# First block's norms on the vector engine, first weights in tiles of their own, and four casts with a fixed place in ScalarE's order

## The chip, the cores and the metric

One NeuronCore of a Trainium2 chip runs the kernel. The metric is the device time of one execution in microseconds. The engines are named as in the profile: PE (TensorE), DVE (VectorE), ACT (ScalarE), POOL (GpSimd) and SP, whose queue issues every DMA of this kernel.

## The reference, cut to what matters

One decoder layer over 2048 tokens of width 1024, in float32:

```python
h = rmsnorm(x, g_mix)                       # x * rsqrt(mean(x^2) + 1e-6) * g_mix
z = h @ w_in                                # 1024 x 4352: r|k|v, three loras, pool, two gates
z_rwkv = token_shift(z[..., :1792], mu)     # z + (z_prev - z) * mu
y_a = rwkv7_mix(z_rwkv, ...) @ w_out_a      # loras, delta-rule state, group norm
y_b = multiscale_pool_mix(z_pool) @ w_out_b
x = x + (gate_a * y_a + gate_b * y_b) @ w_o
x = x + square(relu(rmsnorm(x) @ w_ff1)) @ w_ff2
x = x + sigmoid(rmsnorm(x) @ w_pg) * (p @ w_pe)
return rmsnorm(x, g_final)
```

The change touches the first two lines, for the first 512 tokens.

## The kernel before

The tokens are cut into four blocks of 512. `stage_A(b)` norms a block, turns it (transposes it through PE into `big`), multiplies it by `w_in` in column blocks of 128 and works the results up; `stage_B(b)` does the two output projections; the MLP and the embedding follow. Between the dense work run the recurrent units (`prep`, `chain`, `gnorm`). They read what `stage_A` stored in `zD`, and the first may begin when block 0's twelve r, k, v column blocks are stored.

A float32 product is made of three products of halves (`mm3`): a tile is split into a high half, which ACT makes by a rounding copy ("CAST" in the profile), and a low half, the difference, which DVE or POOL makes. `transpose_split` does it for the turned input, `wtile` for the weights: it loads a 512 KB column block into a `wr` tile (four buffers), casts it into a `wf` tile (three buffers, L241) and subtracts (L244, DVE 384 columns, POOL 640). With `keep` it also stores the split block and enters it in the table `wcache`, so that a later block loads it ready made. For block 0 that is done for column blocks of even number.

Ahead of `stage_A` the first block's four tiles of 128 tokens are loaded into the same four `wr` buffers and normed (L214 to L225): ACT sums the squares, `rstd` is 13 small operations on DVE, and the scaling follows. For x0 and x1 DVE does it in one operation (L222); for x2 and x3 POOL multiplies by the gain `gmix` (L224) and DVE by the statistic (L225). The first weights, column block 12, are then asked for by `wtile` (all of their low half on POOL). They take the `wr` buffer of x0, so their load waits until x0 has been turned.

The order of work: PE's instructions stand in program order. Those of the other engines and of SP are ordered by the library, by priority (program order) and by a simulated time line of the kernel. In `stage_A(0)` the program order is: turn x0 and x1; first half (256 tokens) of column block 12; turn x2 and x3; turn the small vectors (`fill_vec`); second half of block 12; its shift, tanh and casts into `yx`; block 13; its shift, tanh and cast into `yx`; then blocks 0 to 11, each with a small lora product and a tanh behind it. The blocks are generators, and `wtile` is called for a block when its generator is first advanced, after the lines that stand before it have been traced:

```python
            zl = yield from shifted(12, 12)        # block 12: product, copy out (L457), shift
            ...
                ACT.copy(out=yx[on, 0, i, :], in_=src[on])                     # L472, twice
            zl = yield from shifted(13, 13)        # calls wtile for block 13 first
            ...
            ACT.copy(out=yx[:, 0, 2, :], in_=zl)                               # L478
            for zi, m in enumerate(zorder):
                zs = yield from shifted(zi, m)     # calls wtile for block m first
                ...
                    ACT.activation(out=lo, in_=ps, func=AF.Tanh, ...)          # L491
```

Of the kernel before, what the change touches and what calls it, by code (L numbers as in the profile page):

```python
# [10 lines left out]
F32 = mybir.dt.float32  # L11
FR = mybir.dt.float32r
# [3 lines left out]
ALU = mybir.AluOpType  # L16
AX = mybir.AxisListType

P = 128
# [14 lines left out]
TB = 512  # L34
# [64 lines left out]
def hybrid_kernel(ctx, tc, consts, x, p, g_mix, w_in, mu_shift, w0, w_decay_up, a0, w_aaa_up,  # L99
                  w_gate_up, k_k, k_a, r_k, ln_x_w, ln_x_b, pool_w, pool_scale, b_gates,  # L100
                  w_out_a, w_out_b, w_o, g_mlp, w_ff1, w_ff2, g_ple, w_ple_gate, w_ple_proj,
                  g_final, out, stop=None, dbg=None):
    nc = tc.nc
    PE, ACT, DVE, POOL, SP = nc.tensor, nc.scalar, nc.vector, nc.gpsimd, nc.sync
# [5 lines left out]
    dram = ctx.enter_context(tc.tile_pool(name="dram", bufs=1, space=bass.MemoryType.DRAM))  # L110
# [6 lines left out]
    const = ctx.enter_context(tc.tile_pool(name="const", bufs=1, side="left"))  # L117
# [26 lines left out]
    def rsqrt(pool, src, n, tag, iters=3, rows=P, bufs=2):  # L144

        y = pool.tile([rows, n], F32, name=f"rs_y{tag}", bufs=bufs)
        h = pool.tile([rows, n], F32, name=f"rs_h{tag}", bufs=bufs)
        q = pool.tile([rows, n], F32, name=f"rs_q{tag}", bufs=bufs)
        DVE.tensor_scalar(y.bitcast(I32), src.bitcast(I32), 1, None, op0=ALU.logical_shift_right)
        DVE.tensor_scalar(y.bitcast(I32), y.bitcast(I32), -1.0, MAGIC, op0=ALU.mult, op1=ALU.add)  # L150
        DVE.tensor_scalar(h, src, -0.5, None, op0=ALU.mult)
        for _ in range(iters):
            DVE.tensor_tensor(q, y, y, ALU.mult)
            DVE.tensor_tensor(q, q, h, ALU.mult)
            DVE.scalar_tensor_tensor(y, q, 1.5, y, op0=ALU.add, op1=ALU.mult)
        return y

    def sumsq(pool, xt, ss, junk_kw):
        junk = pool.tile([P, D], BF16, name="junk", **junk_kw)
        ACT.activation(out=junk, in_=xt, func=AF.Square, accum_out=ss)  # L160

    def rstd(pool, ss, n, tag):

        ms = pool.tile([P, n], F32, name=f"nms{tag}", bufs=2)
        DVE.tensor_scalar(ms, ss, 1.0 / D, 1e-6, op0=ALU.mult, op1=ALU.add)
        return rsqrt(pool, ms, n, tag)
# [34 lines left out]
    with ExitStack() as c1:  # L201
        fg = c1.enter_context(tc.tile_pool(name="fg", bufs=1, side="left"))
        c1r = ExitStack()
        const = c1r.enter_context(tc.tile_pool(name="const1", bufs=1, side="left"))

        def load_x(b, j):
            xt = fg.tile([P, D], F32, name="xt", tag="wr", bufs=WR)
            SP.dma_start(out=xt, in_=xv[b * TB + j * P:b * TB + (j + 1) * P, :])
            return xt


        gbc = const.tile([P, D], F32, name="gmix")
        xnext = {}
        for j in range(4):  # L214
            xnext[0, j] = load_x(0, j)
            if j == 0:
                SP.dma_start(out=gbc, in_=g_mix[0].unsqueeze(0).broadcast_to([P, D]))
            r = fg.tile([P, 1], F32, name="xss0", bufs=4)
            sumsq(fg, xnext[0, j], r, dict(tag="t2k", bufs=5))
            r = rstd(fg, r, 1, "n")  # L220
            if j < 2:
                DVE.scalar_tensor_tensor(xnext[0, j], xnext[0, j], r, gbc, op0=ALU.mult, op1=ALU.mult)  # L222
            else:
                POOL.tensor_tensor(xnext[0, j], xnext[0, j], gbc, ALU.mult)  # L224
                DVE.tensor_scalar(xnext[0, j], xnext[0, j], r, None, op0=ALU.mult)  # L225

        wcache = {}

        def wtile(src, k, n, ws=WS, key=None, keep=False):


            if key in wcache:
                wf = fg.tile([P, 2, 1024], FR, name="wf", tag="wf", bufs=3)
                SP.dma_start(out=wf.bitcast(F32), in_=wcache[key])
                return wf.rearrange("p s (k n) -> p s k n", n=n)
            raw = fg.tile([P, 1024], F32, name="wr", tag="wr", bufs=WR)
            rv = raw[:, 0:k * n].rearrange("p (k n) -> p k n", n=n)
            SP.dma_start(out=rv, in_=src)
            wf = fg.tile([P, 2, 1024], FR, name="wf", tag="wf", bufs=3)
            hi = wf[:, 0, 0:k * n]  # L240
            ACT.copy(out=hi, in_=raw[:, 0:k * n])  # L241
            for eng, c in ((DVE, slice(0, ws)), (POOL, slice(ws, 1024))):
                if c.start < c.stop:
                    eng.tensor_tensor(wf[:, 1, c], raw[:, c], hi.bitcast(F32)[:, c], ALU.subtract)  # L244
            if keep:
                wcache[key] = dram.tile([P, 2, 1024], F32, name=f"wc{len(wcache)}")
                SP.dma_start(out=wcache[key], in_=wf.bitcast(F32))
            return wf.rearrange("p s (k n) -> p s k n", n=n)
# [2 lines left out]

            return b == i % 2

        winv = w_in[0].rearrange("(k p) c -> p k c", p=P)
        wpre = wtile(winv[:, :, 12 * P:13 * P], 8, P, 0, ("in", 12 * P), True)

        cst = const.tile([P, C_MK - P], F32, name="cst")
        SP.dma_start(out=cst, in_=consts[:, P:C_MK])
# [50 lines left out]
        for i in range(2):  # L309
            raw = fg.tile([P, RW], F32, name="lraw", tag="t2k", bufs=5)  # L310
# [24 lines left out]
        raw = fg.tile([P, 2 * P], F32, name="craw", tag="t2k", bufs=5)  # L335
# [71 lines left out]
        def stage_A(b, nxt):  # L407
            t0 = b * TB
            hT = big
            def proj(ps, c0, lo_last=False, wf=None, cols=slice(0, TB)):  # L410
                if wf is None:
                    wf = wtile(winv[:, :, c0:c0 + P], 8, P, key=("in", c0), keep=kept(b, c0 // P))
                if lo_last:
                    for w, h in ((0, 0), (1, 0), (0, 1)):
                        for k in range(8):
                            mm(ps[:, cols], wf[:, w, k, :], hT[:, h, k, cols], (w, h, k) == (0, 0, 0), (h, k) == (1, 7))
                            if k % 3 == 2:
                                yield
                    return
                for k in range(8):  # L420
                    mm3(ps, (wf[:, 0, k, :], wf[:, 1, k, :]), (hT[:, 0, k, :], hT[:, 1, k, :]), k == 0, k == 7)
                    yield
# [130 lines left out]
            for m in range(8):  # L553
                if m >= 1:
                    next(ah, None)
                if m < 7 or not to_B:
                    yield from gate_a(m)
                if m < 7 and prods:
                    yield from product(*prods.pop(0))
                elif pend:  # L560
                    pool_tail(*pend.pop(0))
                    yield
                ps = dps()
                for i, _ in enumerate(proj(ps, 3328 + m * P)):
                    if m == 7 and i == 2:
                        next(ah, None)
                    yield
                th = t2k()
                ACT.activation(out=th, in_=ps, func=AF.Tanh, bias=bgh[:, 8 + m:9 + m], scale=0.5)
                while pend:  # L570
                    pool_tail(*pend.pop(0))
                    yield
                if m % 2 == 0:
                    wob = wtile(wbv[:, :, m * P:(m + 2) * P], 4, 2 * P, key=("b", m), keep=kept(b, m // 2))
                prods.append((m, wob, th))
# [677 lines left out]
    raw = f2.tile([P, 1024], F32, name="wr", tag="wr", bufs=3)[:, 0:512].rearrange("p (k n) -> p k n", n=P)  # L1253
# [114 lines left out]
    lo, hi = slice(0, 512), slice(512, D)  # L1368
# [83 lines left out]
    for n, (blk, c, nm) in enumerate(seq):  # L1452
# [25 lines left out]
        for j in range(4):  # L1478
# [7 lines left out]
            s = {k: v[j] for k, v in accs.items()}  # L1486
# [180 lines left out]
```

## Time and profile before

| | |
|---|---|
| median of 3 runs | 3246.0 us (3239.34 to 3246.55) |
| profiled execution | 3245.66 us |
| its span, first to last instruction | 3243.9 us |
| PE busy | 3046.2 us (94%) |
| DVE, ACT, POOL busy | 2478.3, 1393.3, 1232.9 us |
| mean granted clock of PE | 0.974 of full speed |

The span is what the rows below are counted in, from its start. A row of a time line gives start, length, engine, line of the kernel, operation, the tile written and the tiles read, with a count where several were merged; in brackets is the idle time in front of it and what ended it.

### The profile page before, as it was taken

To read this page: it belongs to the slowest core of one execution; us is meant where nothing else is said; L and a number is where in the kernel's file an instruction comes from. 1 tells how busy PE (TensorE), PEld (TensorE's weight loads), DVE (VectorE), ACT (ScalarE), POOL (GpSimd) and SP (SyncE) were. 2 spreads that over 40 slices of the span, in tenths; PEclk is the share of its full clock that TensorE was granted. 3 is DMA by queue.
4 is the path that set the end of the run, shared out by engine and by line. 5 is a ranking of instruction groups with operands and counts; after the bars stand their busy time and mean duration, and the time that the engine had idled before them with its cause. 6 is when DMAs were issued, how large, how long until landed. Compare 5 with 4: busy or idle time off the path is not lost. (4 is left out here: it accounts for less than half of the span.)

```text
span 3243.9 us, 43606 instructions
## 1 busy us (share of the span) xinstructions
PE 3046.2 (94%) x14409; PEld 2487.0 (77%) x14409; DVE 2478.3 (76%) x5419; ACT 1393.3 (43%) x2697; POOL 1232.9 (38%) x1325
## 2 busy tenths in 40 slices
PE   7999998899999998879979999999989999999998
PEld 6777777778787876758768788788768888887787
DVE  4479887788888888985478787866658898888765
ACT  4445654455445544533144444433343335333332
POOL 4555444444343534531125555645422232222100
PEclk9999999999999999989999999999989999999999
DMA  7866767666666666767765556544454456435431
GB/s 245 245 218 209 237 208 229 228 218 207 210 224 208 203 193 221 256 217 253 278 214 170 187 187 227 196 152 150 181 205 145 154 191 220 147 117 178 142 108 69
DMA packets 422846, 636.50 MB, mean 196 GB/s; under 512 B 173726, under 2 KB 286044, under 8 KB 391388
## 3 DMA queue, kind: packets, MB, share of 16 engines
q1 hardware_dynamic: 422620, 633.72, 58.9%
q8 instruction: 114, 1.87, 0.2%
q14 instruction: 112, 0.92, 0.1%
HBM read 439.62 MB, written 193.99 MB: 195 GB/s over the span
## 5 line engine op out<-in xcount | busy, mean ns | idle before, releaser
L133 PE MATMUL d<-big,wf 128*128 128x512 f32 (+1 forms) x3288 | 851.5, 407 | 19.5 <-DVE wf L244 9.4
L133 PEld LDWEIGHTS d<-big,wf 128*128 128x128 f32 x3288 | 610.7, 193 | 158.4 <-DVE wf L244 12.2
L133 PE MATMUL d<-op 128*128 128x512 f32 x1344 | 318.6, 396 | 18.9 <-ACT op L1111 14.8
L1112 POOL TENSOR_TENSOR op<-hr,op 128x1024 fp32r<-128x1024 f32 x56 | 157.2, 2807 | 455.4 <-ACT op L1111 455.4
L133 PEld LDWEIGHTS d<-op 128*128 128x128 f32 x1344 | 254.3, 189 | 78.3 <-ACT op L1111 15.2
L1111 ACT CAST op<-hr 128x1024 fp32r<-128x1024 f32 x112 | 117.7, 1051 | 357.3 <-issue 151.8
L1112 DVE TENSOR_TENSOR op<-w,op 128x1024 fp32r<-128x1024 f32 x112 | 183.6, 1640 | 109.3 <-ACT op L1111 109.3
L872 DVE TENSOR_TENSOR Xtmp<-Xt,At 128x16 f32<-128x16 f32 (+15 forms) x512 | 239.9, 468 | 9.3
L1112 POOL TENSOR_TENSOR op<-wr,op 128x512 fp32r<-128x512 f32 x96 | 145.9, 1521 | 246.7 <-ACT op L1111 246.6
L133 PE MATMUL d<-wf,big 128*128 128x512 f32 x768 | 202.3, 416 | 21.0 <-DVE t2k L611 18.7
L133 PE MATMUL d<-yx,wf 128*128 128x512 f32 x768 | 205.4, 413 | 15.7 <-DVE t2k L611 6.5
L1293 POOL TENSOR_TENSOR t<-t,t 128x512 f32<-128x512 f32 x128 | 192.2, 1511 | 69.0 <-DVE t L1303 31.6
L133 PEld LDWEIGHTS d<-wf,big 128*128 128x128 f32 x768 | 147.6, 198 | 59.7 <-DVE t2k L611 22.9
L133 PE MATMUL d<-wg,op 128*128 128x512 f32 x768 | 184.2, 395 | 4.5 <-ACT wg L1111 3.1
L133 PEld LDWEIGHTS d<-yx,wf 128*128 128x128 f32 x768 | 146.1, 197 | 51.9 <-DVE t2k L611 8.2
L1111 ACT CAST op<-wr 128x512 fp32r<-128x512 f32 x192 | 114.7, 619 | 155.4 <-DMA wr<-in_w_ff_dram 39.8
L133 PEld LDWEIGHTS d<-wg,op 128*128 128x128 f32 x768 | 145.1, 190 | 38.5 <-ACT wg L1111 5.7
L133 PE MATMUL rp<-op 128*128 128x512 f32 x672 | 171.3, 390 | 0.0
L133 PE MATMUL rc<-op 128*128 128x512 f32 x672 | 170.6, 389 | 0.0
L875 DVE TENSOR_REDUCE Xt<-Xtmp 128x8 f32<-128x16 f32 (+15 forms) x512 | 147.4, 288 | 9.2
L244 POOL TENSOR_TENSOR wf<-wr,wf 128x640 fp32r<-128x640 f32 (+2 forms) x69 | 119.9, 1739 | 78.5 <-ACT wf L241 73.1
L133 PEld LDWEIGHTS rp<-op 128*128 128x128 f32 x672 | 126.1, 188 | 26.9
(320 smaller groups left out, 6322.3 us busy)
## 6 DMA issues: line engine op xcount, KB each, us to landing
wf<-wc SPq DMA_DIRECT2D x131, 1024.0 KB, 5.3
wc<-wf SPq DMA_DIRECT2D x50, 1024.0 KB, 6.2
wr<-in_w_ff_dram SPq DMA_DIRECT2D x64, 512.0 KB, 3.8
w<-in_w_ff_dram SPq DMA_DIRECT2D x32, 1024.0 KB, 7.5
wr<-in_w_in_dram SPq DMA_DIRECT2D x51, 512.0 KB, 4.4
zD<-t2k SPq DMA_DIRECT2D x96, 256.0 KB, 3.9
zs<-zD SPq DMA_DIRECT2D x32, 640.0 KB, 6.4
At<-aD SPq DMA_DIRECT2D x32, 512.0 KB, 4.8
```

What stands on the lines that cost most here:

```text
L133: PE.matmul(out_, lhsT, rhs, start=start, stop=stop, **kw)
L244: eng.tensor_tensor(wf[:, 1, c], raw[:, c], hi.bitcast(F32)[:, c], ALU.subtract)
L872: DVE.tensor_tensor(tmp[:, :, :, 0:n], Xt[:, :, 0:n].unsqueeze(2).broadcast_to([P, MCOL, FS, n]), At[:, 0:n, r:n].rearrange("p s r -> p r ...
L875: DVE.tensor_reduce(Xt[:, :, r:n].unsqueeze(3), tmp[:, :, :, 0:n], AX.X, ALU.add)
L1111: ACT.copy(out=dst[0], in_=src)
L1112: eng.tensor_tensor(dst[1], src, dst[0].bitcast(F32), ALU.subtract)
L1293: eng.tensor_tensor(out_, a, b, op)
```

## The change

The four sums of squares are asked for first, and the statistics and scalings come behind them in order: x0, x1, then x2 and x3 with one set of statistics for both. All four scalings are one DVE operation each, and POOL has no part. The weights of column block 12 are loaded in two halves of 256 KB into two tiles of their own (buffers that the `ze` tiles use later), behind x1 on SP's queue; each half is cast by ACT and subtracted by DVE, and the split block is stored and entered in the table as before.

In `wtile`, a cast that is traced while the table holds at most two entries is handed to `tc.keep_in_program_order`. That library function adds one edge of order, from the instruction that was traced last before it on the same engine to this one. The edge fixes the order of issue, and adds no wait of its own. The function's core:

```python
        prev = next((i for i in reversed(cur.bb.instructions)
                     if i is not ins.ins and i.engine == engine), None)
        if prev is not None:
            self.add_manual_dep(ins.ins, prev.name, ...NoSync...)
```

The diff:

```diff
+        winv = w_in[0].rearrange("(k p) c -> p k c", p=P)
+        wraw = [const.tile([P, 15 + TB], F32, name="ze", tag="pl", bufs=3)[:, 0:TB].rearrange("p (k n) -> p k n", n=P)
+                for _ in range(2)]
+        ss0 = [fg.tile([P, n], F32, name=f"xss{i}") for i, n in enumerate((1, 1, 2))]
         for j in range(4):
             xnext[0, j] = load_x(0, j)
             if j == 0:
                 SP.dma_start(out=gbc, in_=g_mix[0].unsqueeze(0).broadcast_to([P, D]))
-            r = fg.tile([P, 1], F32, name="xss0", bufs=4)
-            sumsq(fg, xnext[0, j], r, dict(tag="t2k", bufs=5))
-            r = rstd(fg, r, 1, "n")
-            if j < 2:
-                DVE.scalar_tensor_tensor(xnext[0, j], xnext[0, j], r, gbc, op0=ALU.mult, op1=ALU.mult)
-            else:
-                POOL.tensor_tensor(xnext[0, j], xnext[0, j], gbc, ALU.mult)
-                DVE.tensor_scalar(xnext[0, j], xnext[0, j], r, None, op0=ALU.mult)
+            elif j == 1:
+                for h in range(2):
+                    SP.dma_start(out=wraw[h], in_=winv[:, 4 * h:4 * h + 4, 12 * P:13 * P])
+            sumsq(fg, xnext[0, j], ss0[min(j, 2)][:, max(j - 2, 0):max(j - 1, 1)], dict(tag="t2k", bufs=5))
+        for j, n in ((0, 1), (1, 1), (2, 2)):
+            r = rstd(fg, ss0[j], n, f"n{n}")
+            for i in range(n):
+                DVE.scalar_tensor_tensor(xnext[0, j + i], xnext[0, j + i], r[:, i:i + 1], gbc, op0=ALU.mult, op1=ALU.mult)
...
-            ACT.copy(out=hi, in_=raw[:, 0:k * n])
+            cast = ACT.copy(out=hi, in_=raw[:, 0:k * n])
+            if len(wcache) <= 2:
+                tc.keep_in_program_order(cast)
...
-        wpre = wtile(winv[:, :, 12 * P:13 * P], 8, P, 0, ("in", 12 * P), True)
+        wf = fg.tile([P, 2, 1024], FR, name="wf", tag="wf", bufs=3)
+        wpre = wf.rearrange("p s (k n) -> p s k n", n=P)
+        for h in range(2):
+            ks = slice(4 * h, 4 * h + 4)
+            ACT.copy(out=wpre[:, 0, ks], in_=wraw[h])
+            DVE.tensor_tensor(wpre[:, 1, ks], wraw[h], wpre[:, 0, ks].bitcast(F32), ALU.subtract)
+        wcache["in", 12 * P] = dram.tile([P, 2, 1024], F32, name="wcpre")
+        SP.dma_start(out=wcache["in", 12 * P], in_=wf.bitcast(F32))
```

## Rows read from the trace of the kernel before

**Rows 1.** The page: span, engines' busy time, and one line of DMA issues

```profile
span 3243.9 us, 43606 instructions
...
PE 3046.2 (94%) x14409; PEld 2487.0 (77%) x14409; DVE 2478.3 (76%) x5419; ACT 1393.3 (43%) x2697; POOL 1232.9 (38%) x1325
...
wr<-in_w_in_dram SPq DMA_DIRECT2D x51, 512.0 KB, 4.4
```

**Rows 2.** Busy time by stretches: length, engines (instructions), granted clock, DMA share, GB/s

```profile
0.00:31.00 31.00, 10.71 (x57) 9.68 (x57) 21.63 (x66) 13.39 (x23) 17.14 (x29) 1.00 0.65 214
31.00:81.00 50.00, 50.00 (x228) 41.07 (x228) 17.07 (x28) 25.16 (x38) 20.51 (x25) 1.00 0.84 263
81.00:162.00 81.00, 81.00 (x357) 64.19 (x356) 38.62 (x68) 36.41 (x61) 46.05 (x60) 1.00 0.80 245
```

**Rows 3.** Timeline of all engines, 0 to 32 us

```profile
6.13 0.15 DVE L165 TENSOR_SCALAR nmsn<-xss 128x1 f32<-128x1 f32 x1 [6.13 <-ACT junk L160]
...
8.44 1.28 DVE L222 SCALAR_TENSOR_TENSOR xt<-xt,rs_yn,gmix 128x1024 f32<-128x1024 f32 x1
...
11.00 2.35 POOL L224 TENSOR_TENSOR xt<-xt,gmix 128x1024 f32<-128x1024 f32 x1 [2.38 <-ACT junk L160]
...
11.22 2.15 DVE L153 TENSOR_TENSOR rs_qn<-rs_yn 128x1 f32<-128x1 f32 x1
...
21.73 1.97 PE L137 MATMUL d<-ident,xt 128*128 128x128 f32 x8 [9.97 <-DVE xt L222]
...
23.52 5.02 PE L133 MATMUL d<-big,wf 128*128 128x256 f32 x24
...
28.37 1.47 PE L137 MATMUL d<-ident,xt 128*128 128x128 f32 x12
...
31.17 14.32 PE L133 MATMUL d<-big,wf 128*128 128x256 f32 x72
```

**Rows 4.** Groups by line and shape, 0 to 60 us: busy, mean ns

```profile
L185 DVE TENSOR_TENSOR big<-d,big 128x512 fp32r<-128x512 f32 x8 | 5.3, 685 | 0.3 <-ACT big L184 0.2
...
L225 DVE TENSOR_SCALAR xt<-xt,rs_yn 128x1024 f32<-128x1024 f32 x2 | 1.5, 753 | 0.1
```

**Rows 5.** Timeline of ACT, DVE and PE, 34 to 52 us

```profile
34.39 0.59 ACT L457 COPY ze<-d 128x512 f32<-128x512 f32 x1 [1.22 <-PE d L133]
...
35.45 1.05 ACT L241 CAST wf<-wr 128x1024 fp32r<-128x1024 f32 x1
...
37.05 1.26 ACT L472 CAST yx<-t2k 64x512 fp32r<-64x512 f32 x2
...
39.96 0.59 ACT L457 COPY ze<-d 128x512 f32<-128x512 f32 x1 [1.65 <-PE d L133]
...
42.02 0.63 ACT L476 ACTIVATE t2k<-t2k 128x512 f32<-128x512 f32 x1
...
42.68 1.70 DVE L477 TENSOR_SCALAR t2k<-t2k 128x512 f32<-128x512 f32 x1
...
45.52 0.59 ACT L457 COPY ze<-d 128x512 f32<-128x512 f32 x1 [0.49 <-PE d L133]
...
46.01 5.75 PE L133 MATMUL d<-big,wf 128*128 128x512 f32 x24
...
46.59 1.05 ACT L241 CAST wf<-wr 128x1024 fp32r<-128x1024 f32 x1
...
47.53 0.70 ACT L491 ACTIVATE t2k<-d,vec 128x512 f32<-128x512 f32 x1
```

**Rows 6.** Timeline of PE, behind two idle stretches later on

```profile
188.14 6.95 PE L133 MATMUL d<-big,wf 128*128 128x512 f32 x22 [2.75 <-DVE wf L244]
...
315.48 1.22 PE L133 MATMUL rc<-U,aof 128*128 128x128 f32 x4 [3.02 <-ACT U L907]
...
316.35 6.01 PE L133 MATMUL d<-big,wf 128*128 128x512 f32 x15
```

**Rows 7.** Busy time in one stretch behind the second, columns as in rows 2

```profile
314.60:321.40 6.80, 5.92 (x16) 4.86 (x17) 6.60 (x13) 6.63 (x17) 3.36 (x5) 0.50 0.57 171
```

More of the change, by code (lines that the diff above doesn't have):

```diff
@@ L252, in kept @@
             return b == i % 2
-        winv = w_in[0].rearrange("(k p) c -> p k c", p=P)
-        wpre = wtile(winv[:, :, 12 * P:13 * P], 8, P, 0, ("in", 12 * P), True)
+        wf = fg.tile([P, 2, 1024], FR, name="wf", tag="wf", bufs=3)
[6 more added lines that the diff above has]
+        SP.dma_start(out=wcache["in", 12 * P], in_=wf.bitcast(F32))
         cst = const.tile([P, C_MK - P], F32, name="cst")
```

## The prediction

> **What bounds the kernel now.** I read the page first: TensorE (PE) is busy 3046.2 of 3243.9 us [rows 1], so a change at the start counts only by how much earlier or later PE gets through its fixed order. Then the table by stretches: in the first 31 us PE works 10.71 us, and from 31 to 162 us it does not stop (50.00 of 50, 81.00 of 81) [rows 2]. Whatever moves PE's start of steady work, or opens a hole in those 131 us, moves all that follows, since the recurrent units start only when block 0's columns have been stored.
>
> The timeline says what the start waits for [rows 3]. The reader should see four things. The statistics of one tile keep VectorE (DVE) busy from 6.13 to 8.44 (2.31 us for 13 one-column operations), scaling it takes 1.28. While GpSimd (POOL) multiplies x2 by the gain (11.00, 2.35 us), one of those tiny operations on DVE takes 2.15 us in place of some 0.15. So x1 is turned only at 21.73, after 9.97 us of idle PE, the first half of column block 12 starts at 23.52 and takes 5.02, and x2 and x3 are turned from 28.37. The second half, and steady work with it, starts at 31.17.
>
> Last I followed ScalarE (ACT) through the blocks after it [rows 5]. In front of each block's copy out of PSUM stands a cast made early: the one that starts at 35.45 is for a block that PE reaches after two more copies (39.96, 45.52). That lead is why PE never waits for weights there.
>
> **Part 1: norms and first weights.** Removed: POOL's two gain products (2.35 each), two DVE scalings of 753 ns [rows 4], one set of 13 small operations, POOL's low half of the first weights, and the wait of these weights for x0's buffer. Added: two DVE scalings of 1.28, two ACT casts and two DVE subtractions of 512 columns. Moved: two loads of 256 KB, on SP's queue now behind x1 and so ahead of x2 and x3. At the 263 GB/s of [rows 2], 0.52 MB is 2.0 us, so x2 and x3 land that much later; DVE has work on x0, x1 and the weights until 17.4 (below) and covers it. Without that cover it would cost the 2.0 us. The load of block 13 gets x0's buffer, free at the same time as before. The store of the first weights and the small vectors' loads stay behind that load.
>
> Without POOL, DVE sets the start. Before x3 is scaled it has 3 x 2.31 (statistics, x2 and x3 together), 4 x 1.28 (scalings) and 6 subtractions at 0.69 (four of x0 and x1, two of the weights; [rows 4]): 6.9 + 5.1 + 4.1 = 16.2, so 6.13 + 16.2 = 22.3. Less statistics and scalings of x2 and x3 (4.9) that is the 17.4 above. Then one subtraction frees the PSUM buffer for x3's second half (0.69), four turns at 0.12 (1.47 for 12) and the vectors' turn (0.3) follow: second half of block 12 at 23.8 in place of 31.17, **-7.4 us**. Bounds: PE alone would allow 6.13 + 2 x 3.59 = 13.3 for x1, then 1.79 (21.73 to 23.52), 5.02 and 2.80 (28.37 to 31.17): 22.9, so -8.3. If one collision with POOL (2.2) and the two subtractions of the lora weights (1.4) get ahead, it is 27.4, so -3.8. I take -7.4, with nothing between the terms but DVE's own work.
>
> **Part 2: the pins.** Each pin puts a cast behind the ACT instruction traced last before it. It catches four casts: blocks 13, 0, 1 and 2 (the store table holds 1, 1, 2 and 2 entries when they are traced; at block 3 it holds 3). Which instruction that is follows from the code: `wtile` runs when `proj` is first advanced, and `shifted(13)` is entered after block 12 has been copied out, shifted, put through tanh and cast into `yx`. So the cast of block 13 stands behind the second copy into `yx`, which needs block 12's result, and PE's next instruction needs that cast. The casts of 0, 1 and 2 likewise stand behind the last ACT work of 13, 0 and 1. The lead of [rows 5] is gone for these four, and each hole lies in the stretch where PE did not stop.
>
> Prices, from [rows 5], counted from the start of a block's copy out, when PE is about free. Block 13: the copies into `yx` end 37.05 + 1.26 - 34.39 = 3.92 later, the cast takes 1.05: 5.0, and 0.2 until DVE has the low part that the third matmul wants: 5.2. Block 0: tanh ends 42.02 + 0.63 - 39.96 = 2.69 later; the DVE step took 1.70 beside POOL, but POOL would then be idle, so 0.4 (half of the 753 ns for twice the columns, an estimate); the copy 0.63, the cast 1.05, the low part 0.2: 5.0; with 1.70, 6.3. Blocks 1 and 2: the lora tanh ends 47.53 + 0.70 - 45.52 = 2.71 later, cast 1.05, low part 0.2, less the 0.49 in which PE does the lora products (it goes on at 46.01): 3.5; if the unpinned cast of a later block (46.59) doesn't stand before the tanh as it does now, 2.5. I take 3.0, as nothing shows which. Sum 5.2 + 5.0 + 2 x 3.0 = **+16.2** (14.4 without the low parts, 18.5 with every long form).
>
> Behind a late cast on ACT stands only the copy of the block that needs it. On DVE and POOL its subtraction is late too. On SP the store of block 0's split weights is late, and behind it loads for blocks four ahead, at 4.4 us each from issue to landing, with more than one block in hand: nothing.
>
> **Part 3: the clock after the holes.** At 315.48 PE came back from 3.02 us of idleness; the granted clock was 0.50, the lower level of 1.2 GHz [rows 7], and 15 matmuls took 6.01 us where 24 take 5.75 at the higher [rows 5, 6]: 2.4 lost. After 2.75 us of idleness (188.14) 22 took 6.95 where 5.27 were due: 1.7 lost [rows 6]. Four holes of 2.5 to 5.2 us at 2.0 each: **+8.0** (6.8 to 9.6). The Trainium skill (TensorE: Matmul & The Clock Gate, Terms) reckons such a loss as the throttled time times the missing share of the clock. That would be half of the 6.8 us of [rows 7], 3.4 for each hole, and an estimated 3268 in all; the trace, with 2.4 and 1.7, shows less, because PE is idle in part of the low stretch.
>
> **Sum.** -7.4 + 16.2 + 8.0 = +16.8. The profiled execution took 3245.66 us (span 3243.9 and 1.8 around it), 0.3 under the median of 3246.0: 3245.66 + 16.8 = 3262.5. Bounds of the case: -8.3 + 14.4 + 6.8 = +12.9 (3258.6) and -3.8 + 18.5 + 9.6 = +24.3 (3270.0).
>
> **Rivals.** *The casts come in time* (0.13). If the instruction traced last is the copy of the turned input, as the change's words have it, then the casts of 13 and 0 are done while PE works on block 12, nothing waits, and only part 1 is left: 3245.66 - 7.4 = 3238.3, not slower. It decides where the cast of block 13 starts before block 12's copy out. For it: nothing but a pin makes ACT late there. Against it: the order of the generator's steps.
>
> *The clock holds* (0.07). The holes are there but cost no clock: +8.8, 3254.5. For it: the granted clock stays at 1.00 through the first 162 us [rows 2]. Against it: [rows 6, 7], after shorter holes.
>
> *The delay is taken up later* (0.04). PE idles 197.7 us in all [rows 1]; if later waits shrank by as much, the time would be 3245.7. Against it: those waits are for work that itself begins when block 0 has been stored.
>
> *More is won than the start* (0.03). Over 9.7 us (0.3%) would need more than the 8.3 that PE allows at the start, so another order of DVE's work later on, without the holes: 3234.
>
> That leaves 0.73 for the forecast, of which 0.03 may lie below 3255.7. A difference under 0.3% is about what a measurement of this kernel can't tell from none. Slower 0.70, within 0.3% 0.27 (0.03 + 0.13 + 0.07 + 0.04), faster 0.03. The range: 3245 to 3271 leaves out the first and the last rival (0.16) and the forecast's tail; the forecast's own is 3254 to 3271, from the held clock to the upper bound.
>
> **What would show it.** Part 1: the second half of block 12 starts at 22.9 to 27.4; no POOL product of x; no one-column DVE operation over 1 us before 17. Part 2: the wait table of the first 100 us names the casts of weights as what PE waited for, four times, about 5, 5, 3 and 3 us; on ACT the cast of 13 follows the copies into `yx`. Part 3: granted clock 0.5 just behind these holes. After the fourth hole the blocks follow at 5.75 us again, and the rest is the old trace, later by some 17 us. I am wrong if the cast of 13 lies before block 12's copy out, or if later stretches differ by more than a few us.

## The result, and the profile after

The changed kernel takes 3267.76 us in the median of four runs (3267.19 to 3278.65) against 3246.28 us of the kernel before, measured beside it; the ratio on record is 1.0087, with a 95% interval of 1.007 to 1.0104. It is slower, as forecast, but by more than the forecast's 16.8 us. The medians lie 21.5 us apart, which would be inside the range; the ratio puts the time at 1.0087 x 3246.28 = 3274.5 us, above the 3271 at which the range ended. Four runs are few, and one of them lies 10 us above the others; a repeat, below, has a ratio of 1.0071. The profiled execution took 3268.2 us, 22.5 more than the one of before.

The page first, span and busy time, as in [rows 1]:

```profile
span 3266.4 us, 43588 instructions
...
PE 3060.3 (94%) x14409; PEld 2492.8 (76%) x14409; DVE 2482.4 (76%) x5408; ACT 1391.8 (43%) x2698; POOL 1216.4 (37%) x1322
```

The same stretches as in [rows 2]. The second was full before and is not now; PE's granted clock there is 0.80 in the mean:

```profile
0.00:31.00 31.00, 13.96 (x81) 12.66 (x81) 18.21 (x60) 13.39 (x26) 8.42 (x26) 1.00 0.77 250
31.00:81.00 50.00, 36.65 (x121) 27.84 (x122) 13.58 (x16) 17.16 (x25) 15.06 (x16) 0.80 0.43 130
81.00:162.00 81.00, 81.00 (x351) 64.63 (x350) 26.57 (x40) 32.02 (x51) 39.27 (x51) 1.00 0.83 256
```

Who waited for whom, PE in the first 120 us: what was waited for, us in total, times, longest. Before there was no wait for a cast in this stretch:

```profile
PE d L133 <- ACT wf L245: 13.5, 4, 4.8
PE d L137 <- DVE nmsn L165: 10.0, 1, 10.0
PE d L137 <- DVE xt L229: 4.7, 1, 4.7
PE d L137 <- DVE big L185: 2.1, 1, 2.1
```

PE's timeline, which answers to the PE rows of [rows 3, 5]:

```profile
16.68 1.97 PE L137 MATMUL d<-ident,xt 128*128 128x128 f32 x8 [4.75 <-DVE xt L229]
18.48 4.93 PE L133 MATMUL d<-big,wf 128*128 128x256 f32 x24
23.24 1.47 PE L137 MATMUL d<-ident,xt 128*128 128x128 f32 x12
26.83 0.66 PE L137 MATMUL d<-ident,xt 128*128 128x128 f32 x4 [2.12 <-DVE big L185]
...
27.63 3.17 PE L133 MATMUL d<-big,wf 128*128 128x256 f32 x24
35.29 7.84 PE L133 MATMUL d<-big,wf 128*128 128x512 f32 x24 [4.49 <-ACT wf L245]
47.97 8.28 PE L133 MATMUL d<-big,wf 128*128 128x512 f32 x24 [4.84 <-ACT wf L245]
...
59.03 7.54 PE L133 MATMUL d<-big,wf 128*128 128x512 f32 x24 [2.08 <-ACT wf L245]
...
69.40 7.55 PE L133 MATMUL d<-big,wf 128*128 128x512 f32 x24 [2.14 <-ACT wf L245]
...
77.48 5.78 PE L133 MATMUL d<-big,wf 128*128 128x512 f32 x24
```

The reader should see three things. The second half of block 12 starts at 27.63, 3.54 earlier than before. In front of blocks 13, 0, 1 and 2 stand four holes, 13.55 us together, and each of these blocks takes 7.5 to 8.3 us where it took 5.75. Block 3 starts at 77.48; in the trace of before it starts here:

```profile
58.57 5.76 PE L133 MATMUL d<-big,wf 128*128 128x512 f32 x24
```

So the kernel is 18.91 us behind at block 3. That number, read at the same matmul in every trace, is what the experiments are compared by. It does not contain what the rest of the kernel adds (22.5 - 18.9 = 3.6 us here), which varies more from run to run.

ACT's timeline shows the pins as the prediction had them, with one exception:

```profile
30.84 0.59 ACT L470 COPY ze<-d 128x512 f32<-128x512 f32 x1 [2.61 <-PE d L133]
...
33.55 0.61 ACT L485 CAST yx<-t2k 64x512 fp32r<-64x512 f32 x1
34.19 1.04 ACT L245 CAST wf<-wr 128x1024 fp32r<-128x1024 f32 x1
35.14 0.61 ACT L485 CAST yx<-t2k 64x512 fp32r<-64x512 f32 x1
...
46.36 0.62 ACT L491 CAST yx<-t2k 128x512 fp32r<-128x512 f32 x1 [0.49 <-DVE t2k L490]
46.88 1.04 ACT L245 CAST wf<-wr 128x1024 fp32r<-128x1024 f32 x1
```

The cast of block 13 (34.19) comes 3.35 us after block 12's copy out began (30.84), between the two casts into `yx`: the edge is drawn from the one traced last, so that one must have been scheduled ahead of the other. In the trace of before the same cast starts at 27.91, 6.5 us ahead of block 12's copy out (34.39):

```profile
27.91 1.05 ACT L241 CAST wf<-wr 128x1024 fp32r<-128x1024 f32 x1 [1.85 <-DMA wr<-in_w_in_dram]
```

The last view is the clock in blocks 13 and 0, and in the first part of blocks 0 and 1, columns as in [rows 2]:

```profile
35.29:43.13 7.84, 7.84 (x24) 5.92 (x24) 2.49 (x2) 0.47 (x1) 2.51 (x2) 0.72 0.25 69
47.97:56.09 8.12, 8.12 (x24) 6.42 (x25) 0.54 (x1) 0.00 (x0) 2.04 (x2) 0.67 0.65 194
...
47.90:52.00 4.10, 4.03 (x10) 3.16 (x11) 0.56 (x1) 0.02 (x1) 2.04 (x2) 0.50 0.34 128
...
59.00:62.50 3.50, 3.47 (x10) 2.54 (x11) 0.56 (x1) 0.00 (x0) 2.05 (x2) 0.66 0.48 160
```

### The profile page after: what moved, and what is told of

Its sections match the earlier page's. It is cut to its first block, busy times and chain, and to the rows that moved or that the text cites. A ratio compares the mean times of both kernels' runs of the same rounds, so it can differ in the third digit from the quotient of the medians.

```text
span 3266.4 us, 43588 instructions
## 1 busy us (share of the span) xinstructions
PE 3060.3 (94%) x14409; PEld 2492.8 (76%) x14409; DVE 2482.4 (76%) x5408; ACT 1391.8 (43%) x2698; POOL 1216.4 (37%) x1322
## 5 line engine op out<-in xcount | busy, mean ns | idle before, releaser
L133 PE MATMUL d<-big,wf 128*128 128x512 f32 (+1 forms) x3288 | 863.6, 411 | 31.0 <-ACT wf L245 21.7
L133 PE MATMUL d<-op 128*128 128x512 f32 x1344 | 318.2, 396 | 18.9 <-ACT op L1124 14.8
L133 PEld LDWEIGHTS rc<-op 128*128 128x128 f32 x672 | 126.1, 188 | 26.2
```

Source lines behind the costliest of these rows:

```text
L133: PE.matmul(out_, lhsT, rhs, start=start, stop=stop, **kw)
```

## Experiments

"Shift" below is the start of block 3 less 58.57 us, in the profiled execution of each run. "Hole" is a wait of PE in front of a block, "pin" one of the four edges. Comments in the diffs are not in the code.

**Is it the pins?** The first run takes them out of the changed kernel, the second puts them alone into the kernel before.

```diff
-            if len(wcache) <= 2:
-                tc.keep_in_program_order(cast)
```

> The changed kernel without the four pins; the rest of the change stays. If the pins are the cost, the four holes (4.49 + 4.84 + 2.08 + 2.14 = 13.55 us) and the low clock behind them (8.9 us) are gone and only the earlier start (-3.5 us) and perhaps the later drift (up to +3.4 us) remain: 3242 to 3246 us. If the new start itself, with other orders on DVE and ACT behind it, is the cost, the time stays above 3260 us.

Measured: 3250.76 us, ratio 1.0009 (0.9999 to 1.002); block 3 starts at 60.16, a shift of +1.6. The time is 5 us above the upper end of what was expected, and far from the 3260 of the rival.

```diff
+            if 1 <= len(wcache) <= 2:
+                tc.keep_in_program_order(cast)
```

> The kernel before with the pins alone, on the casts of blocks 13, 0, 1 and 2. If the pins are the cost: four holes of about 5, 5, 2 and 2 us in front of these blocks, granted clock 0.5 behind each, together about 22 us, 3266 to 3270 us. If the pins only cost together with the new start, under 3255 us.

Measured: 3266.16 us, ratio 1.0058 (1.0042 to 1.0074); PE's waits for casts come to 13.5 us in four again, block 3 starts at 80.62: a shift of +22.1. (In the kernel before `wtile` also casts block 12's weights, while the table is empty; the lower bound leaves that cast out.) The pins are the loss, with the new start or without it. But the first run held a surprise: without pins nothing of the earlier start was left. PE's and ACT's timelines say where it went:

```profile
18.44 4.37 PE L133 MATMUL d<-big,wf 128*128 128x256 f32 x24
22.64 1.47 PE L137 MATMUL d<-ident,xt 128*128 128x128 f32 x12
29.48 1.11 PE L137 MATMUL d<-ident,xt 128*128 128x128 f32 x4 [5.36 <-DVE big L185]
...
30.82 16.18 PE L133 MATMUL d<-big,wf 128*128 128x256 f32 x72
```

```profile
23.37 1.29 ACT L326 CAST lrw<-lraw 128x512 fp32r<-128x512 f32 x2 [3.18 <-DMA lraw<-in_w_aaa_up_dram]
...
27.17 1.04 ACT L245 CAST wf<-wr 128x1024 fp32r<-128x1024 f32 x1 [1.80 <-DMA wr<-in_w_in_dram]
28.12 1.56 ACT L184 CAST big<-d 128x512 fp32r<-128x512 f32 x3
```

x2 was turned from 22.64, but ACT's copies of it start only at 28.12: in front of them stand two groups of casts that wait for their loads, 3.18 and 1.80 us. The second, a cast of weights, is what a pin behind the turned input would take away.

**The edge in the place that the words name.** The cast is held behind the last copy of the turned input:

```diff
-                tc.keep_in_program_order(cast)
+                tc.add_manual_dep(cast.ins, turned[-1].ins.name, ...NoSync...)
...
-            ACT.copy(out=hi, in_=pv3)
+            turned.append(ACT.copy(out=hi, in_=pv3))
```

> The changed kernel with each of the four edges drawn from the last copy of the turned input (the last ACT copy of transpose_split), not from the instruction traced last. If what costs is the place of the edge, no hole is left: 3241 to 3246 us, and the second half of block 12 starts at 27.6 us or up to 1.5 us earlier than without any pin. If any pin costs, because ACT's order is fixed too early, more than 3255 us.

Measured: 3245.94 us, ratio 0.9995 (0.9983 to 1.0006); second half of block 12 at 28.23, block 3 at 57.31, a shift of -1.3. No hole is left. Of the two rivals on what the edges do, this settles it: their place costs, not their being there. The start, at 28.23, is 0.6 us later than expected and no better than with the pins as they were; PE still waits for the turned x2:

```profile
27.43 0.66 PE L137 MATMUL d<-ident,xt 128*128 128x128 f32 x4 [2.83 <-DVE big L187]
...
28.23 15.93 PE L133 MATMUL d<-big,wf 128*128 128x256 f32 x72
```

**One pin, and the other two.** Only the cast of block 13, and only those of blocks 1 and 2:

```diff
-            if len(wcache) <= 2:
+            if key == ("in", 13 * P):                       # one run
+            if key in (("in", P), ("in", 2 * P)):           # the other
```

> The changed kernel with a single pin, on the cast of block 13. If each pin makes its own hole and its own stretch of low clock: one hole of 4.5 us in front of block 13, that block at 7.8 us in place of 5.6, none in front of blocks 0, 1 and 2; at the start of block 3 the shift against the kernel before is 18.9 - 22.5 + 6.8 = about +3 us, and the time 3248 to 3253 us. If one late cast makes those after it late too, more than one hole is left and the shift is over 10 us.

Measured: 3254.71 us, ratio 1.0024 (1.0015 to 1.0033). One hole of 4.49 us, block 3 at 61.86, a shift of +3.3, as the sum had it; the time is 1.7 us above what was expected.

> The changed kernel with pins on the casts of blocks 1 and 2 alone. If these short holes cost as they did beside the long ones: about 2.1 us of waiting each, and each block at 7.5 us in place of 5.75: +7.8 us against the run without pins, which was 1.6 us behind the kernel before at the start of block 3, so a shift of about +9.4 us there, and 3253 to 3258 us. If the low clock there was left from the long holes in front of 13 and 0: +4.2 us, a shift of 5.8.

Measured: 3255.11 us, ratio 1.003 (1.0019 to 1.0041), shift +9.3. The two blocks:

```profile
49.40 7.55 PE L133 MATMUL d<-big,wf 128*128 128x512 f32 x24 [2.08 <-ACT wf L245]
...
59.78 7.54 PE L133 MATMUL d<-big,wf 128*128 128x512 f32 x24 [2.13 <-ACT wf L245]
```

Each pin makes its own hole, and each of these two blocks, behind a hole of 2.1 us, took 7.5 us in place of 5.75. Against the run without pins these two cost 7.7 us at block 3.

The two runs show one thing more. With block 13's pin alone the second half of block 12 starts at 27.61; with the pins of 1 and 2 alone it starts at 31.07, about as late as without pins (30.82), and again ACT waits at a cast of weights (1.92 us) ahead of its copies of x2. So it is the pin on block 13 that keeps a cast of weights from standing there, and most of the start's 3.54 us in the changed kernel is its doing.

**What kept the start from -7.4?** Two causes were seen in the trace: ACT's copies of x2 behind casts of the lora weights, and x1, turned at 16.68 where DVE could have had it at 13.3. The next run has the edges of the third, and traces the loads and casts of the lora weights and of the two small masks behind the turned input, held by the same kind of edge. The run after it also holds four subtractions on DVE behind x1's scaling:

```diff
+                fill_lora()          # loads, casts, subtractions moved here, behind fill_vec()
...
+            tc.add_manual_dep(cast.ins, turned[-1].ins.name, ...NoSync...)     # lora, masks
```

> As the run with the edges from the turned input, and the loads and casts of the lora weights and of the two small masks are traced behind the turned input and held there. If ACT's copies of x2 stood behind casts that waited for their loads (25.47 us, where the turned tile was there at 23.8), PE's wait of 2.1 to 3.1 us before the last turn goes: second half of block 12 at 25.5 to 26.5 us, and block 12 to block 0 at the higher clock (14.3 us in place of 15.9); shift at the start of block 3 of -4 to -6 us. If PE waits there for DVE's subtractions alone, 27.6 to 28.3 us again.

Measured: 3241.81 us, ratio 0.9978 (0.9964 to 0.9993), shift -5.1. ACT copies x2 at 23.05, and PE's wait before the last turn falls to 0.53 us, from 2.83 in the third run (2.12 in the changed kernel):

```profile
23.05 1.56 ACT L186 CAST big<-d 128x512 fp32r<-128x512 f32 x3 [3.78 <-PE d L137]
```

```profile
24.42 0.66 PE L137 MATMUL d<-ident,xt 128*128 128x128 f32 x4 [0.53 <-DVE big L187]
...
25.21 3.18 PE L133 MATMUL d<-big,wf 128*128 128x256 f32 x24
...
53.45 5.78 PE L133 MATMUL d<-big,wf 128*128 128x512 f32 x24
```

The start is 0.3 us earlier than expected and the shift as expected. Blocks 12 to 0 took 15.1 us (25.21 to 40.29), not 14.3. Of these 0.8 us, 0.27 are a wait of PE for the cast of block 13, which now stands behind the lora casts; the rest has no cause shown. The edit moved the lora weights' loads and DVE's two subtractions as well as ACT's casts, so what each of them is worth is not separated.

```diff
-            DVE.tensor_tensor(wpre[:, 1, ks], ...)          # and the low halves of x0
+            low = DVE.tensor_tensor(wpre[:, 1, ks], ...)
+            tc.add_manual_dep(low.ins, scaled[1].ins.name, ...NoSync...)
```

> As the run before it, and on DVE the low halves of the first weights and of x0 are held behind the scaling of x1. If this order is what kept x1 until 16.7 us: x1 is turned at 13.3 to 13.8, the first half of block 12 starts at 15.1 to 15.6, the second at 22.9 to 24.5 (DVE's sum of the prediction gave 23.8); shift at the start of block 3 -6.5 to -8 us, time about 0.2% under the kernel before. If DVE's work as a whole sets the start, the second half of block 12 does not come before 25.5.

Measured: 3243.37 us, ratio 0.9985 (0.9977 to 0.9994), shift -6.0. PE's timeline:

```profile
14.40 1.97 PE L137 MATMUL d<-ident,xt 128*128 128x128 f32 x8 [1.54 <-DVE xt L235]
16.19 4.44 PE L133 MATMUL d<-big,wf 128*128 128x256 f32 x24
21.46 1.82 PE L137 MATMUL d<-ident,xt 128*128 128x128 f32 x12 [0.83 <-DVE xt L235]
...
24.29 3.15 PE L133 MATMUL d<-big,wf 128*128 128x256 f32 x24
```

The second half of block 12 starts at 24.29, 6.9 us earlier than before. PE now waits for x2's scaling (0.83 us), so here DVE's work as a whole is the bound, and its sum, 23.8, is 0.5 off. x1 was turned 0.6 us later than expected, and the shift falls 0.5 short; the start of the second half lies within what was expected. Both of these last kernels are faster than both kernels of the case, by 0.22% and 0.15% against the kernel before; between the two the intervals overlap.

**What the rest of the kernel adds.** The changed kernel and the kernel before, unaltered, twice more each:

> The changed kernel again, unaltered. If the 3.4 us that it lost behind block 2 are chance (the order of PE, and nearly all of the other engines, is the same there), the shift against the kernel before is again 18.9 us where block 3 starts, and another one at the end; the times lie between 3262 and 3270 us. If they follow from the later start, the shift at the end is again 22.3 us.

> The kernel before, unaltered, for a second trace of it. If the few us by which changed kernels drift behind block 2 (from -0.8 to +5 us in the traces so far) are chance, this trace, too, drifts by some us against the first one of the same program, and more in the stretch of the recurrent units than in the MLP. If the program fixes its later waits, the two agree to 1 us throughout.

> The changed kernel for a third trace. Where block 3 starts 18.9 to 21.5 us behind the kernel before. From there to the end two traces lost another 3.4 and 5.1 us. If that belongs to the changed program, this trace loses 3 to 5 us again; if it is chance, it may as well be 0 or negative.

> The kernel before for a third trace. Between the start of block 3 and the end its second trace stood within 0.9 us of the first. If later waits of this program are steady, this one does too; if they are chance, it may differ by 3 to 5 us.

Measured: the changed kernel 3270.99 us, ratio 1.0071 (1.0053 to 1.0089), and 3275.2 us in a single run; the kernel before 3246.92 us, ratio 1.0003 (0.9992 to 1.0013), and 3253.92 us in a single run. Against the first trace of before, in us (the last column is the difference of the spans less the shift):

| trace | block 3 at | shift | span | lost later |
|---|---|---|---|---|
| changed, first | 77.48 | 18.9 | 3266.4 | 3.6 |
| changed, second | 80.10 | 21.5 | 3270.8 | 5.4 |
| changed, third | 81.27 | 22.7 | 3273.4 | 6.8 |
| before, second | 58.30 | -0.3 | 3244.5 | 0.9 |
| before, third | 58.26 | -0.3 | 3252.1 | 8.5 |

The start did not repeat as expected: the changed kernel's own shift varies by 3.8 us, and the median of the repeat, 3270.99, is 1 us above the 3262 to 3270 expected. And for the later part neither clean answer came. The kernel before has traces with 0.9 and 8.5 us more than its first, so 3.6 to 6.8 lies within what one program does by itself; three traces a side don't show whether the change adds to it.

## Why the prediction was right and wrong

**Part 2, the pins: right.** The four casts stand where the prediction put them, but for the one cast into `yx` behind that of block 13, and PE waits for them four times: 4.49, 4.84, 2.08 and 2.14 us where 5.2, 5.0, 3.0 and 3.0 were forecast; 13.55 in place of 16.2. Block 13 was 0.7 less because only one of the two casts into `yx` stood in front. Blocks 1 and 2 took the short form (2.5 with the low part): no cast of a later block came before the lora tanh. The runs without pins, with pins alone and with single pins show cause and size.

**Part 3, the clock: right.** The four blocks took 31.2 us (7.84 + 8.28 + 7.54 + 7.55) where 23.0 are due, 8.2 more; 8.0 was forecast. Behind the hole of 4.84 us the granted clock is 0.50 over the first 4.1 us; behind that of 2.08 it is 0.66 in the mean of the first 3.5. The Trainium skill (TensorE: Matmul & The Clock Gate, Terms) takes such a loss as the throttled time times the missing share of the clock, half at the lower level. In block 0 the mean granted clock is 0.67 over 8.12 us, so two thirds of it, 5.4 us, were at the lower level, and half of that is 2.7; the trace has 8.28 - 5.75 = 2.5, and agrees here, where PE was busy throughout. Parts 2 and 3 together: 24.2 forecast, 18.91 + 3.54 = 22.45 measured. The 3268 that the prediction names beside its sum lies next to the median by chance: it has 13.6 us for the clock, where 8.2 were lost, and the same -7.4 for the start.

**Part 1, the start: the direction right, the size wrong, and this is the step that failed.** The prediction took "-7.4, with nothing between the terms but DVE's own work". It measured -3.5, -2.8 and -2.8 in the three traces (27.63, 28.33 and 28.33 in place of 31.17), outside the bound of -3.8, and most even of that is the pin on block 13: without pins the second half of block 12 started at 30.82, 0.35 earlier than before, and block 3 1.6 later. DVE's total was nearly right: x3 was scaled by 21.19, where the sum had 22.3. What failed is the overlap. The sum let DVE's total set the start and left x1 at the 13.3 of its lower bound, as if DVE's order served PE's and ACT had nothing in front of x2. DVE's timeline of the changed kernel:

```profile
9.98 1.51 DVE L266 TENSOR_TENSOR wf<-ze,wf 128x512 fp32r<-128x512 f32 x2
...
13.08 0.69 DVE L185 TENSOR_TENSOR big<-d,big 128x512 fp32r<-128x512 f32 x1 [0.56 <-ACT big L184]
...
15.35 1.28 DVE L229 SCALAR_TENSOR_TENSOR xt<-xt,rs_yn,gmix 128x1024 f32<-128x1024 f32 x1
```

The weights' and x0's subtractions went in between x1's statistics, so x1 was scaled by 16.63 and not by 13.3. From there PE's own steps (1.79, 4.9, 2.8) lead to 26.2. The missing 1.4 us are ACT's. It had stood idle for 4.02 us, to 23.30, at a cast of lora weights whose load had not landed; that cast and the three groups behind it (the second half of the lora weights, the two masks) then held it until the copies of x2 at 25.47, while the turned x2 was ready from about 23.8.

```profile
23.30 0.62 ACT L329 CAST lrw<-lraw 128x512 fp32r<-128x512 f32 x1 [4.02 <-DMA lraw<-in_w_aaa_up_dram]
...
25.47 1.56 ACT L184 CAST big<-d 128x512 fp32r<-128x512 f32 x3
```

The prediction named the lora weights' subtractions on DVE, but not their casts on ACT. The Trainium skill's page TensorE: Matmul & The Clock Gate (Architectural detail) calls ScalarE and VectorE strict first-in, first-out. The trace without pins agrees: there ACT stood idle for 1.80 us at a cast whose load had not landed, with the copies of x2, turned from 22.64, behind it. The two runs that put these orders right show the cause: against 28.23 with the edges from the turned input alone, the second half starts at 25.21 when the lora work is moved too, and at 24.29 with DVE's order as well.

**The sum and the range.** At block 3 the forecast was +16.8, and +18.9, +21.5 and +22.7 were measured: in the first trace the start made 3.9 more, the holes and the clock 1.7 less. Behind block 3 the forecast had nothing; 3.6 more came there, and whether that is the change's doing stays open, as the table shows. The range left 1 us above its upper bound; it made nothing of how far the same program's times lie apart, 3238.57 to 3257.16 us over all runs of the kernel before, nor of what PE's wait at the start does to the clock of block 12 (below). With a start of -2.8 and 2.3 for that, the upper bound would have been -2.8 + 18.5 + 9.6 + 2.3 = +27.6, 3273.3.

**The rivals.** "The casts come in time" is what the third experiment made of the kernel, and it came to 3245.94, not 3238.3, because the start was 2.9 us earlier, not 7.4, and from block 12's second half through block 0 the matmuls took 15.93 us in place of 14.32. "The clock holds" is refuted by the rows of blocks 13 and 0; what spoke for it, a granted clock of 1.00 from the start on, is doubtful for the first 31 us (below). "The delay is taken up later" is refuted: the rest of the kernel gave nothing back. "More is won than the start" did not happen.

## What to carry to other kernels

An edge that means "behind everything traced so far" is as good as the trace order: find the instruction that stands last before it, and ask what that one waits for. Here it waited for the product whose successor needed the cast, and naming the wanted instruction cost nothing. When one engine's sum is taken for the start of another, write down its order as well, and which of its entries wait for loads: half of the gain lay in the order, not in the work.

## What was not expected of the hardware

The same program ran block 12's second half, the same 24 matmuls, in 3.17, 4.66 and 5.43 us. In front of it PE had waited 2.12, 3.06 and 3.12 us for the turned input. The stretch in the first and the third trace of the changed kernel, columns as in [rows 2]:

```profile
27.63:30.80 3.17, 3.17 (x25) 2.96 (x24) 1.41 (x7) 0.60 (x2) 0.00 (x0) 1.00 0.71 200
```

```profile
28.33:33.76 5.43, 5.43 (x25) 5.19 (x24) 1.06 (x6) 0.51 (x2) 0.00 (x0) 0.52 0.36 102
```

The granted clock was 1.00 in the one and 0.52 in the other. Of the 3.8 us by which the changed kernel's shift varied, 2.3 are these matmuls and 0.7 the later start.

The length of the wait alone does not say what follows. Behind 2.12 us here, and 2.16 in the run with block 13's pin alone, the 24 matmuls took 3.17 and 3.18 us; behind holes of 2.08 and 2.13 in front of blocks 1 and 2 the blocks took 7.55 and 7.54 in place of 5.75. Nor does a longer wait cost more: in three runs without holes in front of blocks 13 and 0 PE waited 2.83, 5.36 and 5.92 us for the last turn, and from block 12's second half through block 0 the matmuls took 15.93, 16.18 and 15.56 us. What decides it is not shown.

One figure of the profile needs care. In [rows 2] the granted clock of the first 31 us is 1.00, but the durations there do not bear it out. In the trace of before, at a stated 1.00, 20 of the matmuls of block 12's first half took 3.80 us:

```profile
24.00:27.80 3.80, 3.80 (x20) 3.80 (x20) 3.30 (x10) 2.04 (x6) 0.00 (x0) 1.00 0.74 226
```

The whole half took 5.02 us, against 3.17 for the same shape and number in the row from 27.63 above, and 5.43 at 0.52.
